# The order of the output products and the state products in the third step of a chunk of RWKV-7 time mixing

## The chip, the cores and the metric

The kernel runs on one core of a Trainium2 chip (trn2). The metric is the device time of one execution in microseconds (us). Engines are named as the profile names them: PE is TensorE's matmuls, PEld its weight loads, DVE is VectorE, ACT is ScalarE, POOL is GpSimd, SP is SyncE, which issues DMAs.

## What is computed

The reference is a trunk of two layers on 256 tokens of width 2048: a layer of RWKV-7 time mixing with a squared-ReLU MLP, then a layer of band attention with another MLP. The change lies in the time mixing alone. For each of 32 heads of 64 channels a 64 by 64 state S runs over the tokens, and each token reads it:

```python
def step(S, inp):
    r_t, w_t, k_t, v_t, kk_t, a_t = inp
    sa = jnp.einsum('bhvk,bhk->bhv', S, -kk_t)
    S = (S * w_t[:, :, None, :] + sa[..., None] * (kk_t * a_t)[:, :, None, :]
         + v_t[..., None] * k_t[:, :, None, :])
    y = jnp.einsum('bhvk,bhk->bhv', S, r_t)
    return S, y
```

`y` is then normalized per head, gated, and projected by `w_o`.

## The kernel before

**Chunks in place of tokens.** Two heads fill 128 partitions and make a pair; there are 16 pairs. The 256 tokens are cut into four chunks of 64 (`c` = 0 to 3). Within a chunk the recurrence is solved with matrices: `early` makes decays and scaled keys, `invert` builds and inverts a triangular 64 by 64 matrix per chunk (32 by 32 products at line 111, transposes on VectorE at line 239, sums at 254), and `late` (line 266) walks through the four chunks in order, since each needs the state that the chunk before left.

**The three steps of a chunk in `late`.** Each `yield` ends a step.

- First step: `g` = `mk`·`vp` (line 280) plus, from the second chunk on, the old state's part `kr`·`zs` (line 283). ScalarE copies `g` out (284).
- Second step: the inverse times `g` (287). ScalarE copies it out, negated, as `sa` (288).
- Third step: the new state and the output. The state, for chunks 0 to 2: `bk`·`vp` (293) and `bk`·`sa` (295) add up in one place, and VectorE makes `zs` from it: a plain copy in chunk 0 (298), the old state times the decay `pc` plus the products in chunks 1 and 2 (300). The output of the chunk: `vp`·`mk` (304), the old state times `kr` from chunk 1 on (307), and `sa`·`ar` (309) add up in `py`.

Every product is done for the two heads of the pair, one after the other.

**Where the results lie.** One tile `lt` (line 271, two buffers, so two pairs have one each) holds everything of a pair's `late`. It has 128 partitions and 2 × 256 float32: the first half holds `pch`, in which `g`, the second step's result and the state's products have 64 columns each, and the second half holds `py`, 64 columns for each chunk. Thus the state's products, which `zs` reads, and the output lie in the two halves of one tile.

**What sets the order on TensorE.** Slots (line 871 on). In each slot every live pair does one step: first the pairs that are in `invert`, then those in `late`, the oldest first, then those in `early`. Two pairs are in `late` at a time, 8 steps apart. Then come four blocks of the dense projections of a later pair (`proj_steps`; lines 412 and 413, 512 and 256 columns wide), or of the output projection in the last slots (401 to 403). Three slots in four end with a step of the modulation (`ada`, line 454: VectorE adds a 128 by 1024 tile that a DMA brought). A block under `tc.issue_after(x)` gets an order: its instructions on the engine of `x` stand behind `x` in that engine's queue. With it each pair's step is put behind the last TensorE instruction of the one before, and the dense blocks behind the last step. In the third step, line 302 puts the output products behind the last state product:

```python
with b.tc.issue_after(ins.ins) if c < 3 else nullcontext():
    for K in heads:
        mm(ch(py)[K, c, :], vp[K, c, :], mk[K, c, C:P], start=True, stop=False)
```

**What else VectorE does meanwhile.** Dense weights arrive as float32 and are split into two halves, the high one by ScalarE (378) and the low one by VectorE (381, 128 by 1024 elements each); three buffers of each. VectorE also does most of `early` (lines 132 to 185), the masks of `invert` (212, 227, 263) and the modulation's sums (454). It works its queue in order.

**Waits between engines** are put in by the framework where two instructions touch the same tile.

## Time and profile before

| what | value |
|---|---|
| median of three runs | 2723.46 us (2720.56 to 2725.22) |
| the profiled execution, time | 2723.2 us |
| the profiled execution, span | 2721.4 us |
| mean granted TensorE clock | 0.989 |
| PE busy | 2614.4 us |
| DVE busy | 2104.5 us |
| ACT busy | 1345.5 us |
| first to last product of line 304 | 287.3 to 764.6 us |

The span goes from the first to the last instruction of the program. The profile gives, for groups of instructions of one line, engine and shape, the count, the busy time, the mean duration, and behind a second bar the idle time of the engine just before them with what ended it. In a table of waits, "A <- B: t, n, m" reads: A's engine stood idle for t us in n places, m the longest, until B was done. `out<-in` are the names of tiles. Matmuls are pipelined, so that rows of TensorE overlap by up to some tenths of a microsecond. A float32 product of 64 by 64 shows as two instructions.

### The profile page before, as it was taken

The numbers are of one execution on the slowest core, as the hardware profiler recorded it, in microseconds if no ns is written. First come the engines' busy times: TensorE is split into PE (matmuls) and PEld (weight loads), VectorE is DVE, ScalarE is ACT, GpSimd is POOL, SyncE is SP. The second block draws the span as 40 slices with busy tenths as digits, with TensorE's granted clock in tenths as the row PEclk, the third lists the DMA queues.
The fourth block names the chain that finished last, engine by engine and source line by source line (L and its number), as shares of the span: only waits on it lengthen the run. The fifth ranks groups of instructions, "written<-read, shape, count | busy, mean of one in ns | idle before, by whom it ended". The sixth has DMA issues, their size and how long they took to land.

```text
span 2721.4 us, 58341 instructions
## 1 busy us (share of the span) xinstructions
PE 2614.4 (96%) x23690; PEld 2233.9 (82%) x23690; DVE 2104.5 (77%) x3109; ACT 1345.5 (49%) x2432; POOL 200.1 (7%) x320
## 2 busy tenths in 40 slices
PE   6999899889999999999999999999999999999997
PEld 3777677777789888888888898877898888888886
DVE  5778778777878988888888898899988555556555
ACT  3345444445456535446355554465565364453554
POOL 0002222222110000000000100000100000000002
PEclk8999999999999999999999999999999999999999
DMA  9966545554686989988899769987857555555553
GB/s 332 315 227 214 175 158 186 177 162 154 210 278 212 327 325 331 344 320 310 310 326 327 254 207 323 334 273 256 289 185 269 188 189 187 187 186 192 187 187 123
DMA packets 217390, 662.64 MB, mean 243 GB/s; under 512 B 21408, under 2 KB 68896, under 8 KB 217120
## 3 DMA queue, kind: packets, MB, share of 16 engines
q1 hardware_dynamic: 215056, 656.36, 70.0%
q8 instruction: 186, 3.05, 0.5%
q10 hardware_dynamic: 2064, 2.54, 0.3%
q14 instruction: 84, 0.69, 0.1%
HBM read 656.72 MB, written 2.10 MB: 242 GB/s over the span
## 4 chain that ended last, share of the span: by engine, by line
PE 69%; DVE 1%; DMA 1%; issue 0%; ACT 0%; DVEq 0%; ACTq 0%; SPq 0%
PE pj L412 41%; PE pj L413 21%; PE pj L402 2%; PE pj L401 2%; PE pj L403 2%; DMA rada<-w_ada 1%; PE m L476 0%; PE pT L1102 0%; DVE acc L454 0%; PE po L1109 0%; DVE wL L381 0%; PE S L1081 0%; PE o L401 0%; PE S L1080 0%; PE o L403 0%; PE o L402 0%
## 5 line engine op out<-in xcount | busy, mean ns | idle before, releaser
L381 DVE TENSOR_TENSOR wL<-raw,wH 128x1024 fp32r<-128x1024 f32 x772 | 939.7, 1218 | 355.2 <-ACT wH L378 347.5
L378 ACT CAST wH<-raw 128x1024 fp32r<-128x1024 f32 x772 | 805.9, 1045 | 825.4 <-PE pj L412 666.1
L412 PE MATMUL pj<-aHL,wH 128*128 128x512 f32 x3328 | 1205.8, 404 | 2.2 <-DVE x L927 1.4
L413 PE MATMUL pj<-aHL,wL 128*128 128x256 f32 x3328 | 938.0, 282 | 0.4 <-DVE wL L381 0.4
L412 PEld LDWEIGHTS pj<-aHL,wH 128*128 128x128 f32 x3328 | 631.1, 190 | 155.2 <-issue 9.4
L412 PE MATMUL pj<-hHL,wH 128*128 128x512 f32 x2048 | 721.4, 398 | 0.0
L413 PEld LDWEIGHTS pj<-aHL,wL 128*128 128x128 f32 x3328 | 631.5, 190 | 3.1 <-issue 0.8
L413 PE MATMUL pj<-hHL,wL 128*128 128x256 f32 x2048 | 573.5, 280 | 0.0
L412 PEld LDWEIGHTS pj<-hHL,wH 128*128 128x128 f32 x2048 | 384.5, 188 | 93.7 <-DVE hHL L973 0.2
L413 PEld LDWEIGHTS pj<-hHL,wL 128*128 128x128 f32 x2048 | 386.6, 189 | 0.1
L454 DVE SCALAR_TENSOR_TENSOR acc<-rada,ct,acc 128x1024 f32<-128x1024 f32 x256 | 327.5, 1279 | 9.4 <-DMA rada<-w_ada 8.9
L518 POOL TENSOR_TENSOR ss<-ss,sq 128x256 f32<-128x256 f32 x56 | 54.6, 975 | 1590.8 <-ACT sq L517 1590.5
L998 DVE SCALAR_TENSOR_TENSOR x<-pj,mod,x 128x256 f32<-128x256 f32 x256 | 123.3, 482 | 58.1 <-PE pj L413 54.4
L454 DVE SCALAR_TENSOR_TENSOR acc<-raw,ct,acc 128x1024 f32<-128x1024 f32 x104 | 136.7, 1315 | 27.3 <-DMA raw<-w_ada 27.0
L401 PE MATMUL pj<-aHL,wH 128*128 128x258 f32 x384 | 109.0, 284 | 0.0
L402 PE MATMUL pj<-aHL,wH 128*128 128x258 f32 x384 | 108.9, 284 | 0.0
L403 PE MATMUL pj<-aHL,wL 128*128 128x258 f32 x384 | 108.0, 281 | 0.0
L970 ACT ACTIVATE t<-t 128x256 f32<-128x256 f32 x112 | 46.8, 418 | 122.9 <-DVE t L942 122.9
L403 PEld LDWEIGHTS pj<-aHL,wL 128*128 128x128 f32 x384 | 73.2, 191 | 0.2
L402 PEld LDWEIGHTS pj<-aHL,wH 128*128 128x128 f32 x384 | 72.6, 189 | 0.1
L401 PEld LDWEIGHTS pj<-aHL,wH 128*128 128x128 f32 x384 | 72.2, 188 | 0.2
L304 PE MATMUL lt<-mk,vp 64*64 64x64 f32 x256 | 21.9, 247 | 42.8 <-DVE zs L300 30.2
(244 smaller groups left out, 2849.2 us busy)
## 6 DMA issues: line engine op xcount, KB each, us to landing
raw<-w_up SPq DMA_DIRECT2D x256, 512.0 KB, 4.0
raw<-w_down SPq DMA_DIRECT2D x256, 512.0 KB, 4.2
rada<-w_ada SPq DMA_DIRECT2D x209, 512.0 KB, 5.7
raw<-w_ada SPq DMA_DIRECT2D x111, 512.0 KB, 4.4
rawa<-w_ada SPq DMA_DIRECT2D x64, 512.0 KB, 6.6
rada<-w_ada_kv SPq DMA_DIRECT2D x64, 512.0 KB, 6.2
raw<-w_k SPq DMA_DIRECT2D x32, 512.0 KB, 4.3
raw<-w_r SPq DMA_DIRECT2D x32, 512.0 KB, 4.6
```

The costliest lines, as they stand in the source:

```text
L304: mm(ch(py)[K, c, :], vp[K, c, :], mk[K, c, C:P], start=True, stop=False)
L378: nc.scalar.copy(Hf, raw)
L381: eng.tensor_tensor(out=Lf, in0=raw, in1=Hf, op=ALU.subtract)
L401: nc.tensor.matmul(ps, H[:, i, :], a(kt)[:, 0, :], start=(first and kt == 0), stop=False)
L402: nc.tensor.matmul(ps, H[:, i, :], a(kt)[:, 1, :], start=False, stop=False)
L403: ins = nc.tensor.matmul(ps, L[:, i, :], a(kt)[:, 0, :], start=False, stop=(last and kt == KT - 1))
L412: nc.tensor.matmul(ps, H[:, i, :], a(kt), start=(kt == 0), stop=False)
L413: ins = nc.tensor.matmul(ps[:, 0, :], L[:, i, :], a(kt)[:, 0, :], start=False, stop=(kt == KT - 1))
L454: nc.vector.scalar_tensor_tensor(out=self.acc, in0=raw, scalar=ck, in1=self.acc, op0=ALU.mult, op1=ALU.add)
L518: (eng or nc.gpsimd).tensor_tensor(out=self.ss, in0=self.ss, in1=sq, op=ALU.add)
L970: nc.scalar.activation(t, t, AF.Relu)
L998: nc.vector.scalar_tensor_tensor(out=x, in0=ps[:, i, :], scalar=self.mods[(layer, 5)][:, n:n + 1], in1=x, op0=ALU.mult, op1=ALU.add)
```

## The change

In the third step of chunks 0 to 2 the output's three groups of products come first, and the state's two products second, with an `issue_after` that puts them behind the last output product. Between the two state products the order is swapped as well (`sa` first, `vp` second). `zs` is made on VectorE by the same instruction as before, after the state's products. The variable that held the old state is no longer needed, since `zs` is replaced at the end of the step. In chunk 3 the output products stand alone, as before. The number of instructions, their shapes, the tiles and their buffers are the same.

```diff
             yield
-            old = zs
+            for K in heads:
+                mm(ch(py)[K, c, :], vp[K, c, :], mk[K, c, C:P], start=True, stop=False)
+            if c:
+                for K in heads:
+                    mm(ch(py)[K, c, :], zs[K, :], kr[K, c, C:P], start=False, stop=False)
+            for K in heads:
+                ins = mm(ch(py)[K, c, :], sa[K, :], ch(ar)[K, c, :], start=False, stop=True)
             if c < 3:
-                for K in heads:
-                    mm(pch[K, 2, :], bk[K, 1, c, :], vp[K, c, :], start=True, stop=False)
-                for K in heads:
-                    ins = mm(pch[K, 2, :], bk[K, 0, c, :], sa[K, :], start=False, stop=True)
-                zs = pw.tile([P, C], F32, tag="zs", bufs=4, name="zs")
+                with b.tc.issue_after(ins.ins):
+                    for K in heads:
+                        mm(pch[K, 2, :], bk[K, 0, c, :], sa[K, :], start=True, stop=False)
+                    for K in heads:
+                        mm(pch[K, 2, :], bk[K, 1, c, :], vp[K, c, :], start=False, stop=True)
+                zn = pw.tile([P, C], F32, tag="zs", bufs=4, name="zs")
                 if c == 0:
-                    nc.vector.tensor_copy(zs, pch[:, 2, :])
+                    nc.vector.tensor_copy(zn, pch[:, 2, :])
                 else:
-                    nc.vector.scalar_tensor_tensor(out=zs, in0=old, scalar=pc[:, c, :], in1=pch[:, 2, :],
+                    nc.vector.scalar_tensor_tensor(out=zn, in0=zs, scalar=pc[:, c, :], in1=pch[:, 2, :],
                                                    op0=ALU.mult, op1=ALU.add)
-            with b.tc.issue_after(ins.ins) if c < 3 else nullcontext():
-                for K in heads:
-                    mm(ch(py)[K, c, :], vp[K, c, :], mk[K, c, C:P], start=True, stop=False)
-                if c:
-                    for K in heads:
-                        mm(ch(py)[K, c, :], old[K, :], kr[K, c, C:P], start=False, stop=False)
-                for K in heads:
-                    mm(ch(py)[K, c, :], sa[K, :], ch(ar)[K, c, :], start=False, stop=True)
+                zs = zn
             yield
```

## The prediction

> **What bounds the kernel now.** I read the page first, for the share of each engine; then the table by stages; then the waits of TensorE in the stage that the change touches; then the order of time around single waits.

> The page's head, its busy row and its row of granted clock:

> ```profile
> span 2721.4 us, 58341 instructions
> ...
> PE 2614.4 (96%) x23690; PEld 2233.9 (82%) x23690; DVE 2104.5 (77%) x3109; ACT 1345.5 (49%) x2432; POOL 200.1 (7%) x320
> ...
> PEclk8999999999999999999999999999999999999999
> ```

> TensorE (PE) is busy 96% of the span. The changed lines run from about 287 to 765 us, so I cut the span there (columns: length, then busy us and instructions of each engine, granted clock, share of the DMA engines, GB/s):

> ```profile
> 270.00:770.00 500.00, 449.18 (x8937) 368.10 (x8937) 387.03 (x712) 230.36 (x646) 106.72 (x161) 0.97 0.55 177
> 770.00:2721.40 1951.40, 1932.33 (x12557) 1687.64 (x12555) 1522.52 (x2008) 1002.58 (x1577) 67.17 (x122) 1.00 0.73 256
> ```

> In the time-mixing stage TensorE idles 500.0 − 449.2 = 50.8 us, at a clock of 0.97, while VectorE (DVE) has 113 us free and the DMAs move 177 GB/s where the later stages move 256. After it TensorE is busy 99%. So time saved in the stage should reach the end. Weight loads and modulation steps are issued by count and not by time, so none of them is skipped or added.

> Nearly all of that idle time has one cause. TensorE's waits in the stage (total, times, longest):

> ```profile
> PE lt L304 <- DVE zs L300: 30.2, 29, 3.3
> PE lt L304 <- DVE zs L298: 12.6, 15, 2.1
> PE iv L111 <- DVE tt L239: 7.0, 7, 4.5
> ```

> 44 of the 48 third steps with a state (three chunks of 16 pairs) stop at line 304, for 42.8 us in all. Line 304 multiplies `mk` by `vp` and needs no `zs`. It shares one thing with the VectorE instruction that makes `zs`: the tile `lt`, whose first half zs reads and whose second half 304 writes. The same step in the order of time, once long and once of middle length (us of start, length; the bracket is the idle time before; each x4 is two heads' products in two instructions each):

> ```profile
> 330.77 0.33 PE L293 MATMUL lt<-vp,bk 64*64 64x64 f32 x4
> 330.94 0.28 PE L295 MATMUL lt<-sa,bk 64*64 64x64 f32 x4
> 334.32 0.33 PE L304 MATMUL lt<-mk,vp 64*64 64x64 f32 x4 [3.10 <-DVE zs L300]
> ...
> 338.43 0.33 PE L280 MATMUL lt<-vp,mk 64*64 64x64 f32 x4
> ...
> 365.87 0.33 PE L304 MATMUL lt<-mk,vp 64*64 64x64 f32 x4 [1.14 <-DVE zs L300]
> ...
> 366.36 0.50 PE L412 MATMUL pj<-aHL,wH 128*128 128x512 f32 x1
> ...
> 368.61 0.33 PE L280 MATMUL lt<-vp,mk 64*64 64x64 f32 x4
> ```

> VectorE in the first of these two:

> ```profile
> 330.94 0.28 DVE L254 TENSOR_TENSOR u<-u,iv 128x128 f32<-128x128 f32 x1
> 331.33 1.17 DVE L227 TENSOR_TENSOR u<-u,csts 128x128 f32<-128x128 f32 x1
> 332.42 0.49 DVE L239 STREAM_TRANSPOSE tt<-u 128x128 f32<-128x128 f32 x2
> 332.84 1.24 DVE L454 SCALAR_TENSOR_TENSOR acc<-raw,ct,acc 128x1024 f32<-128x1024 f32 x1
> 334.00 0.27 DVE L300 SCALAR_TENSOR_TENSOR zs<-zs,pc,lt 128x64 f32<-128x64 f32 x1
> ```

> zs itself takes 0.27 us. The rest of the 3.10 is work of other pairs and of the modulation that stood ahead of it in VectorE's queue. TensorE has its next dense products ready and stands still.

> **The change, part by part.** *Moved on TensorE.* The three groups of lines 304, 307 and 309 go ahead of 293 and 295. No instruction is added or dropped, none issues a DMA, and nothing passes a queue other than TensorE's and, behind it, VectorE's. The new first product must wait for what 293 waits for today, the scalar copy `sa` out of the same tile, a step earlier. That wait is nothing (idle before it, after the last bar: 0.0; line 280 stands here for later):

> ```profile
> L280 PE MATMUL lt<-vp,mk 64*64 64x64 f32 x256 | 19.8, 230 | 0.0
> ...
> L293 PE MATMUL lt<-vp,bk 64*64 64x64 f32 x192 | 15.3, 236 | 0.0
> ```

> The swap of the two state products costs nothing: both have had their inputs for a step.

> *Removed: the wait at 304.* −42.8 us. What is late next is zs for the first product of the same pair's next chunk, line 280. From 304 to that 280 TensorE has 368.61 − 365.87 = 2.74 us of other work (the output products, the dense products, the inverse of another pair). That is the cover. Of the 44 waits only two are longer, this 3.10 and the 3.3 of the table of waits; they keep 0.36 and 0.56, so 0.9 us comes back there.

> *Removed with it: clock.* Stretches at half clock follow the long waits. Three of the seven that begin within 1.7 us of the end of such a wait (the first, the fifth and the last), the sum over all seven, and the wait ahead of the fifth:

> ```profile
> 335.02:338.43 3.41, 3.41 (x56) 2.62 (x56) 1.04 (x3) 1.62 (x3) 1.77 (x3) 0.50 0.49 154
> ...
> 546.65:550.06 3.41, 3.41 (x24) 2.64 (x19) 1.28 (x1) 0.37 (x1) 0.00 (x0) 0.50 0.60 202
> ...
> 713.90:717.31 3.41, 3.41 (x72) 3.00 (x72) 1.28 (x4) 1.31 (x3) 0.00 (x0) 0.50 0.16 60
> sum 23.89, PE 23.55 PEld 18.93 DVE 12.71 ACT 7.06 POOL 10.35; mean PE 3.36 PEld 2.70 DVE 1.82 ACT 1.01 POOL 1.48
> ```

> ```profile
> 546.17 0.33 PE L304 MATMUL lt<-mk,vp 64*64 64x64 f32 x4 [1.45 <-DVE zs L298]
> ```

> What one costs is read from the two steps above: 304 to 280 takes 338.43 − 334.32 = 4.11 us with such a stretch inside and 2.74 without, so 1.37 us; seven make 9.6 us.

> [...]

> *Added: a later zs.* The three output groups take 366.36 − 365.87 = 0.49 us, and zs can start that much later, 48 times: at most 23.5 us on VectorE, if it always stood ready for zs. Nothing on TensorE sees it inside the cover of 2.74. Below zero it cannot go, since zs never comes earlier in the step. Queued behind zs on VectorE stand the weights' low halves (line 381), the modulation sums (454) and the inverse's transposes (239); TensorE waits for the last of these, 7.0 us today.

> *Given back: VectorE is tighter.* Its work does not shrink while the stage does. Its own waits in the stage:

> ```profile
> DVE wL L381 <- ACT wH L378: 26.2, 16, 2.7
> DVE acc L454 <- DMA raw<-w_ada: 24.7, 15, 4.4
> DVE u L254 <- PE iv L111: 14.5, 10, 3.3
> ```

> Without 42.8 + 9.6 = 52.4 us the stage would be 447.6 long. Work and DMA waits alone are 387.0 + 24.7 = 411.7, 92% of that. A queue so full will be late somewhere. How much of the gain returns is the term I have to choose. It is bounded below by the 0.9 above, and above by all of it. What guides me is the shape of the 44 waits. 23 of them last 0.31 to 0.51 us, 9.8 in all; the first and the last of the 23:

> ```profile
> 287.31 0.48 PE L304 MATMUL lt<-mk,vp 64*64 64x64 f32 x4 [0.39 <-DVE zs L298]
> ...
> 747.13 0.33 PE L304 MATMUL lt<-mk,vp 64*64 64x64 f32 x4 [0.51 <-DVE zs L298]
> ```

> That is little more than zs's own 0.27 and the hand-over, so VectorE had nothing queued ahead of it, and these cannot come back under a cover of 2.74. The other 21 sum to 42.8 − 9.8 = 33.0. A single one is covered too, but the lag that TensorE's stop used to clear now stays in the queue, and two in a row can exceed the cover. I let a third return, 11.0 us, and two of the seven half-clock stretches with it, 2 × 1.37 = 2.7.

> *The sum.* 42.8 + 9.6 − 11.0 − 2.7 = 38.7 us less. The profiled execution took 2723.2 us, 1.8 more than its span; the median of the three runs is 2723.46, 0.3 above it. 2723.46 − 38.7 = 2684.8; I say 2685.

> **The rivals.** *VectorE becomes the bound.* Say that none of its waits for data and casts shrinks, that each later zs costs it in full, and that its waits for the inverse's products stay: 387.0 + 24.7 + 26.2 + 23.5 + 14.5 = 475.9 us for the stage, a gain of 24, so 2699. For it: 92% above. Against: the casts themselves wait for TensorE to free a weight buffer, 63.2 of their 78.6 us, and that should shrink as TensorE runs on:

> ```profile
> L378 ACT CAST wH<-raw 128x1024 fp32r<-128x1024 f32 (+1 forms) x63 | 64.6, 1025 | 78.6 <-PE pj L412 63.2 <-PE o L402 10.7 <-DMA raw<-w_o 3.4
> ```

> *The wait only moves.* Line 280 of the next chunk writes the same tile that zs reads, so it must wait for zs as 304 does now; if VectorE's queue is always as late, the 42.8 us appear at 280 and at 111, the stretches at half clock stay, and the time stays 2723. [...] Against the rival stands the cover, which 42 of 44 waits fit into. That the order on TensorE stays as it was would give the same time; the new program names the order of the two blocks outright, so I give that little.

> *Slower.* VectorE runs in order. If it stands at zs waiting for products that now come 0.49 us later, 381, 454 and 239 behind it come later too, and the inverse's next product (line 111) and 280 pay. With every old wait back at 280 and all 48 delays passed on: 2723.5 + 23.5 = 2747. It decides from the point at which zs lags its products by more than 2.74 us in most chunks; in this trace 2 of 48 do. VectorE stood at zs for line 295 only 8 times:

> ```profile
> DVE zs L300 <- PE lt L295: 3.1, 8, 0.8
> ```

> **How the numbers follow.** A measurement of this kernel can tell about 0.2%, 5.4 us, from no change. The forecast, a gain of 30 to 52 us: 0.62. VectorE the bound, a gain of 6 to 30: 0.24. The wait moves, within 5.4 us: 0.07. Slower: 0.07. So faster 0.86, same 0.07, slower 0.07. The low end is the whole 52.4 without any return, 2671, and 3 us below for the waits at line 111, 7.0 us today, of which some could go with the rest: 2668. The high end is past the VectorE rival's own 2699, to a gain of 15.5, which leaves out about a third of that case: 2708. About 0.8 of the chance lies inside.

> **What would show it.** On TensorE the order in a third step should read output products, `sa` product, `vp` product, and no idle time at the first of them. The row of waits at the old line 304 should be gone. Line 280's wait for zs and line 111's for `tt` should together be new by about 11 us, and hold no single wait over 2 us except a few. The clock of the stage should go from 0.97 to about 0.99. VectorE's busy time in the stage should stay at 387 us in some 461 us. The stages after it should keep their 1951 us. I am wrong if line 280 shows 44 waits of about a microsecond, if VectorE's idle time at zs for its products grows from 3.1 towards 23 us and TensorE's waits at 111 with it, or if the stage shrinks and the later stages grow by as much.

## The result, and the profile after

| | before | after |
|---|---|---|
| median, same chip | 2722.01 us (4 runs) | 2672.84 us (4 runs) |
| ratio | 1 | 0.9817, 95% interval 0.9800 to 0.9834 |
| span of the profiled execution | 2721.4 us | 2672.0 us |
| granted clock, whole span | 0.989 | 0.994 |

The change makes the kernel 49 us faster. The prediction was 2685 us with a range of 2668 to 2708.

The page of the changed kernel, its busy row and clock row:

```profile
PE 2600.1 (97%) x23690; PEld 2225.4 (83%) x23690; DVE 2101.0 (79%) x3109; ACT 1343.9 (50%) x2432; POOL 209.7 (8%) x320
...
PEclk9999999999999999999999999999999999999999
```

The instructions are the same in number, and every engine's busy time is nearly what it was. To see where the time went I cut both spans at the first and the last product into the tile `lt`; the stretch between them is called the stage from here on. The table by stages of the kernel before, then of the changed one (length, then busy us and instructions of PE, PEld, DVE, ACT and POOL, granted clock, share of the DMA engines, GB/s):

```profile
276.10:765.10 489.00, 439.00 (x8766) 359.04 (x8755) 379.61 (x697) 225.28 (x634) 102.04 (x155) 0.97 0.54 176
765.10:2721.40 1956.30, 1937.23 (x12592) 1692.38 (x12592) 1524.09 (x2011) 1004.55 (x1582) 67.17 (x122) 1.00 0.73 256
```

```profile
274.20:710.00 435.80, 421.18 (x8758) 348.25 (x8755) 374.73 (x696) 224.01 (x634) 111.60 (x155) 0.99 0.60 197
710.00:2672.00 1962.00, 1942.19 (x12593) 1695.04 (x12592) 1525.16 (x2013) 1004.51 (x1582) 67.26 (x122) 1.00 0.73 256
```

The stage is 489.0 − 435.8 = 53.2 us shorter. TensorE's idle time in it goes from 50.0 to 14.6 us, and its busy time from 439.0 to 421.2. What came before the stage is 1.9 us shorter, what comes after it 5.7 longer: 53.2 + 1.9 − 5.7 = 49.4.

TensorE's waits after, from 270 to 720 us:

```profile
PE iv L111 <- DVE tt L239: 8.7, 8, 4.2
PE ms L324 <- DVE s L154: 1.9, 5, 0.8
PE ms L324 <- issue: 1.4, 1, 1.4
PE lt L280 <- DVE zs L307: 1.2, 4, 0.3
```

The 42.8 us of the old line 304 (now 291) are gone. Its successor in the argument, line 280's wait for zs, is 1.2 us in all 48 places together. One step in the order of time, TensorE and then VectorE:

```profile
297.31 0.28 PE L291 MATMUL lt<-mk,vp 64*64 64x64 f32 x4
297.43 0.28 PE L294 MATMUL lt<-kr,zs 64*64 64x64 f32 x4
297.55 0.28 PE L296 MATMUL lt<-ar,sa 64*64 64x64 f32 x4
297.66 0.28 PE L300 MATMUL lt<-sa,bk 64*64 64x64 f32 x4
297.78 0.28 PE L302 MATMUL lt<-vp,bk 64*64 64x64 f32 x4
297.99 0.50 PE L412 MATMUL pj<-aHL,wH 128*128 128x512 f32 x1
...
300.24 0.33 PE L280 MATMUL lt<-vp,mk 64*64 64x64 f32 x4
```

```profile
297.96 0.28 DVE L254 TENSOR_TENSOR u<-u,iv 128x128 f32<-128x128 f32 x1
298.27 0.51 DVE L239 STREAM_TRANSPOSE tt<-u 128x128 f32<-128x128 f32 x2
298.70 0.77 DVE L145 TENSOR_TENSOR_SCAN s<-csts,s 128x256 f32<-128x256 f32 x1
299.39 0.25 DVE L307 SCALAR_TENSOR_TENSOR zs<-zs,pc,lt 128x64 f32<-128x64 f32 x1
```

VectorE is no quicker with zs than it was: here it starts 299.39 − 298.06 = 1.33 us after the end of the products. Over the 48 steps zs is done 0.92 us after that end on average before, and 1.34 us after. But TensorE goes from the last state product to the dense products within 0.21 us, and when it comes to line 280 at 300.24, zs has been done since 299.64.

### The profile page after: what moved, and what is told of

Same layout as the page of the kernel before. It is cut to its first block, busy times and chain, and to the rows that moved or that the text cites. A ratio compares the mean times of both kernels' runs of the same rounds, so it can differ in the third digit from the quotient of the medians.

```text
span 2672.0 us, 58365 instructions
## 1 busy us (share of the span) xinstructions
PE 2600.1 (97%) x23690; PEld 2225.4 (83%) x23690; DVE 2101.0 (79%) x3109; ACT 1343.9 (50%) x2432; POOL 209.7 (8%) x320
## 3 DMA queue, kind: packets, MB, share of 16 engines
q10 hardware_dynamic: 2064, 2.54, 0.3%
## 5 line engine op out<-in xcount | busy, mean ns | idle before, releaser
L381 DVE TENSOR_TENSOR wL<-raw,wH 128x1024 fp32r<-128x1024 f32 x772 | 940.9, 1220 | 342.6 <-ACT wH L378 337.8
L378 ACT CAST wH<-raw 128x1024 fp32r<-128x1024 f32 x772 | 805.5, 1045 | 801.2 <-PE pj L412 646.0
L412 PE MATMUL pj<-aHL,wH 128*128 128x512 f32 x3328 | 1201.9, 403 | 2.0 <-DVE x L927 1.1
L412 PEld LDWEIGHTS pj<-aHL,wH 128*128 128x128 f32 x3328 | 629.5, 189 | 154.1 <-issue 9.2
L412 PE MATMUL pj<-hHL,wH 128*128 128x512 f32 x2048 | 724.6, 399 | 0.0
L412 PEld LDWEIGHTS pj<-hHL,wH 128*128 128x128 f32 x2048 | 384.8, 188 | 95.7 <-DVE hHL L973 0.2
L413 PEld LDWEIGHTS pj<-hHL,wL 128*128 128x128 f32 x2048 | 387.0, 189 | 0.1
L454 DVE SCALAR_TENSOR_TENSOR acc<-rada,ct,acc 128x1024 f32<-128x1024 f32 x256 | 327.5, 1279 | 8.4 <-DMA rada<-w_ada 7.5
L454 DVE SCALAR_TENSOR_TENSOR acc<-raw,ct,acc 128x1024 f32<-128x1024 f32 x104 | 136.4, 1312 | 15.5 <-DMA raw<-w_ada 15.4
L402 PE MATMUL pj<-aHL,wH 128*128 128x258 f32 x384 | 109.0, 284 | 0.0
L970 ACT ACTIVATE t<-t 128x256 f32<-128x256 f32 x112 | 46.8, 418 | 122.6 <-DVE t L942 122.6
L402 PEld LDWEIGHTS pj<-aHL,wH 128*128 128x128 f32 x384 | 72.6, 189 | 0.1
L972 ACT ACTIVATE t<-t 128x256 f32<-128x256 f32 x128 | 53.4, 417 | 3.4
```

What stands on the lines that cost most here:

```text
L378: nc.scalar.copy(Hf, raw)
L381: eng.tensor_tensor(out=Lf, in0=raw, in1=Hf, op=ALU.subtract)
L402: nc.tensor.matmul(ps, H[:, i, :], a(kt)[:, 1, :], start=False, stop=False)
L412: nc.tensor.matmul(ps, H[:, i, :], a(kt), start=(kt == 0), stop=False)
L413: ins = nc.tensor.matmul(ps[:, 0, :], L[:, i, :], a(kt)[:, 0, :], start=False, stop=(kt == KT - 1))
L454: nc.vector.scalar_tensor_tensor(out=self.acc, in0=raw, scalar=ck, in1=self.acc, op0=ALU.mult, op1=ALU.add)
```

## The experiments

Theory: the old stop is made by the shared tile, TensorE stands at the head of its queue while VectorE is late, and any order that puts 2.7 us of other TensorE work between the state products and the next product into that tile takes the stop away, with its loss of clock. Rivals: the order itself matters (what is early or late in the step), the stop is one for data, or the gain is limited by VectorE's total work.

No run leaves out any of the computation. The times are medians in us. The stage's figures are cut as above; half clock is the time in the stage at which the clock stood at half. They are of one execution of each kernel, and the half-clock time differs between executions: the granted clock over the whole span is 0.987 to 0.993 in those of the kernel before, 0.992 to 0.995 in those of the changed one.

| run | time | ratio to before, 95% interval | stage | TensorE idle in it | half clock |
|---|---|---|---|---|---|
| before | 2721 to 2724 | 1 | 489.0 | 50.0 | 30.7 |
| after | 2672.8 | 0.9817 (0.9800 to 0.9834) | 435.8 | 14.6 | 6.8 |
| c0_only | 2718.8 | 0.9982 (0.9972 to 0.9992) | 479.4 | 42.8 | 34.1 |
| c12_only | 2692.8 | 0.9890 (0.9870 to 0.9910) | 454.1 | 26.6 | 17.1 |
| no_swap | 2674.0 | 0.9817 (0.9801 to 0.9833) | 436.6 | 15.8 | 6.8 |
| next_first | 2738.3 | 1.0052 (1.0034 to 1.0071) | 500.2 | 60.4 | 30.7 |
| half_cover | 2699.5 | 0.9924 (0.9909 to 0.9939) | 461.1 | 23.1 | 13.7 |
| cross | 2682.5 | 0.9859 (0.9838 to 0.9881) | 448.1 | 22.3 | 13.7 |
| defer | 2674.5 | 0.9823 (0.9807 to 0.9839) | 439.7 | 18.9 | 3.4 |
| before_zs4 | 2867.0 | 1.0525 (1.0504 to 1.0546) | 630.8 | 135.6 | 184.3 |
| after_zs4 | 2714.3 | 0.9966 (0.9952 to 0.9980) | 475.6 | 41.3 | 34.1 |
| after_dup | 2684.8 | 0.9867 (0.9850 to 0.9883) | 444.2 | 22.2 | 10.2 |
| after_again | 2676.6 | 0.9833 (0.9819 to 0.9847) | 436.5 | 15.6 | 6.8 |
| act_copies | 2668.2 | 0.9799 (0.9784 to 0.9813) | 427.2 | 9.0 | 0 |

### Is it the tile or the order? cross

```diff
-        bank = pp.tile([P, 2, T], F32, tag="lt", bufs=2, name="lt")
-        pch, py = bank[:, 0, 0:3 * C].rearrange("p (a t) -> p a t", a=3), bank[:, 1, :]
+        banks = [b.lts[j % 2], b.lts[1 - j % 2]]
+        pch, py = banks[0][:, 0, 0:3 * C].rearrange("p (a t) -> p a t", a=3), banks[1][:, 1, :]
...
+            self.lts = [pp.tile([P, 2, T], F32, tag=f"lt{i}", bufs=1, name="lt") for i in range(2)]
```

> The old order on TensorE, but a pair's state products and its output lie in two different tiles (of two tiles, each holds one pair's first half and the other pair's second half). If the shared tile made the wait, the waits at line 304 for zs go without any change of order, 42.8 us to under 5, and the half-clock stretches with them; new waits between the two pairs that now share a tile may cost up to about 1 us for each pair's last steps, 16 us: 2672 to 2692 us. If the old order itself is the cause, the waits at 304 stay and the time is 2722 us.

The order in the third step is that of the kernel before. TensorE's waits:

```profile
PE iv L111 <- DVE tt L239: 8.7, 7, 4.5
PE lt L280 <- DVE sl L320: 8.3, 6, 3.7
PE lt L304 <- ACT sa L288: 4.3, 10, 0.4
```

No wait for zs is left at line 304, and the time falls to 2682.5 without any product being moved. So the shared tile makes the stop. The two other rows are the price expected: two pairs now share a tile, and one pair waits for ScalarE or VectorE to read the other's half.

### Is it the work between? next_first and half_cover

Both take the changed kernel and issue line 280 of the next chunk earlier; from the second chunk on it no longer stands in its old place.

```diff
...
+                with b.tc.issue_after(ins.ins):
+                    for K in heads:
+                        mm(pch[K, 0, :], mk[K, c + 1, 0:C], vp[K, c + 1, :], start=True, stop=False)
             yield
...
```

> The changed kernel, with the next chunk's product of mk and vp (line 280) issued right behind the state's products, in the same step, ahead of the dense products. It doesn't need zs as data; it writes the half of lt that zs reads, in other columns. If a product into the tile that zs reads has to wait for zs, and the gain comes from the 2.74 us of dense work between, the stops return at this product: about 40 us of waits, half-clock stretches again, 2712 to 2728 us. If the gain came from the output products being early, or the old wait was one for data, it stays near 2673 us.

The moved product is line 313 there. The waits for it:

```profile
PE lt L313 <- DVE zs L308: 34.4, 27, 3.5
PE lt L313 <- DVE zs L306: 16.5, 15, 2.2
```

The stop is back in full, at a product that has no use for zs: 50.9 us in 42 places. It is 8.1 us more than the 42.8 of the kernel before, and the time is 2738, 10 us above the range I gave. The output products now stand ahead of the state products and delay zs without hiding it. Without a cover the new order is slower than the old one.

In half_cover the same product stands behind the first half of the slot's dense products:

```diff
-                with tc.issue_after(last):
-                    for _ in range(todo):
-                        next(dense, None)
+                for i in range(max(todo, 1)):
+                    with tc.issue_after(last):
+                        if i < todo:
+                            next(dense, None)
+                    last = self.last_pe()
+                    if i == 0:
+                        for first in self.between:
...
```

> As next_first, but the next chunk's product of mk and vp stands in the middle of the slot's dense products, behind the first two of four blocks (about 0.7 us of them) in place of none. In the changed kernel zs is done 0.55 to 2.76 us after the start of the last state products; with a cover of about 0.95 us the parts of these times above it sum to about 33 us, less where another pair's step adds cover. So the waits at this product should fall from 51 us to 20 to 35, and the time lie between the changed kernel and next_first, 2698 to 2720 us. If the wait depended on the order alone and not on the cover, it would be that of next_first, 2738, or of the changed kernel, 2673.

```profile
PE lt L313 <- DVE zs L308: 10.6, 12, 1.4
PE lt L313 <- DVE zs L306: 1.8, 4, 0.5
```

12.4 us, less than the 20 to 35 expected: from the start of the last state product to the moved product TensorE has 1.31 us of work on average (1.05 to 2.67) and not the 0.95 I took. With the cover going from none over half to whole, the wait goes 50.9, 12.4, 1.2. The time of 2699.5 is higher than that wait explains: TensorE's busy time in the stage is 438.0 against 421.2. One part is two more stretches at half clock. The rest lies where the dense run is cut in two. From the start of the instruction before the moved product to the start of the one behind it takes 0.49 us on average, idle time taken out; around line 280 in the changed kernel it is 0.25. Over the 48 that makes 12 us.

### Is it that zs is later, or the swap? defer and no_swap

In defer the state products stay first, and the output products of chunks 0 to 2 go into the next step, behind line 283:

```diff
+                with b.tc.issue_after(ins.ins):
+                    outputs()
             nc.scalar.copy(g, pch[:, 0, :])
...
```

> State products first as in the old order, and the output products of chunks 0 to 2 a whole slot later, behind the first products of the next chunk. It takes the stop away as the change does, by the dense work between, but zs isn't made later. If the later zs costs nothing, the time is that of the changed kernel, 2673 us within 5; if the 0.49 us of later zs is felt (up to 23.5 us in 48 steps), it is faster than the changed kernel by several us.

In no_swap the changed kernel adds `vp`'s product first and `sa`'s second:

```diff
-                        mm(pch[K, 2, :], bk[K, 0, c, :], sa[K, :], start=True, stop=False)
+                        mm(pch[K, 2, :], bk[K, 1, c, :], vp[K, c, :], start=True, stop=False)
...
-                        mm(pch[K, 2, :], bk[K, 1, c, :], vp[K, c, :], start=False, stop=True)
+                        mm(pch[K, 2, :], bk[K, 0, c, :], sa[K, :], start=False, stop=True)
```

> The changed kernel, but with the state's two products in their old order (vp first, sa second). Both have their inputs a step earlier, so my theory expects no difference from the changed kernel: 2673 us within 3. If the swap were part of the gain (sa's product standing first so that something is freed earlier), it would be some us slower.

2674.5 and 2674.0 against 2672.8: both are the changed kernel's time. Where the cover holds, zs half a microsecond later costs nothing, and a wholly different way to the same cover gives the same gain.

### Do the parts add? c0_only and c12_only

The new order stands under `if c == 0:` in one kernel and `if c in (1, 2):` in the other; the old order stands in the `else`.

> The new order in chunk 0 alone; chunks 1 and 2 keep the old one. If each wait is a stop of TensorE for its own zs, and half-clock stretches belong to the waits ahead of them, the parts add up: the 15 waits for line 298 go (12.6 us) and two of the seven stretches (2 x 1.37 us), a gain of about 15 us, near 2707 us, with the waits of chunks 1 and 2 unchanged at about 30 us. The rival, that VectorE's lag only goes on to the next stop, expects the waits of chunks 1 and 2 to grow by most of the 12.6 and a gain under 6 us.

> The new order in chunks 1 and 2 alone. By the sum of parts the 29 waits for line 300 go (30.2 us) and five half-clock stretches (5 x 1.37 us): a gain of about 37 us, near 2685 us; together with the chunk-0 run it should give the 49 us of the whole change within 5 us. By the rival that the lag goes on to the next stop the 15 waits of chunk 0 grow well above 12.6 us and the gain is under 25.

The waits for zs that are left, of c0_only and then of c12_only:

```profile
PE lt L326 <- DVE zs L322: 31.9, 29, 2.8
```

```profile
PE lt L326 <- DVE zs L320: 14.8, 15, 2.2
```

The parts do not add. The gains against before are 5 us (2723.9 − 2718.8) and 31, in sum 36, where I expected 15 and 37 and the whole gives 49. In the traces the two stages are 9.6 and 34.9 us shorter, where the whole gives 53.2, so 8.7 us are missing. Of these 4.8 are idle time of TensorE (7.2 + 23.4 against 35.4), most of it the waits for zs that stay and grow by 1.7 and 2.2 us: the lag does go on to the next stop, though by far less than the rival has it. The other 3.9 are busy time (2.4 + 11.5 against 17.8), and there the clock tells. c0_only has taken 12.6 us of waits away and has no fewer half-clock stretches than before (34.1 us against 30.7); c12_only has still three that are not in the changed kernel. The stretches do not belong to certain waits, as I had assumed in counting seven of them. The rest of the 13 us between 36 and 49 lies between executions and is not placed; the ten executions of c0_only have granted clocks from 0.985 to 0.992.

### How much more could VectorE be late? before_zs4, after_zs4 and after_dup

In the first two, the instruction that makes zs is done four times over:

```diff
+                for _ in range(4):
+                    if c == 0:
...
```

> The kernel before with the same instruction done four times over. Here TensorE stands still until zs is done, so each of the 48 stops grows by the three added instructions, about 0.6 us: 29 us more at line 304, and more half-clock stretches at 1.37 us each: 2750 to 2765 us. If the stops were not on the path that sets the end, it stays at 2722 us.

> The changed kernel with the VectorE instruction that makes zs done four times over in place of once (same result): about 3 x 0.2 us more on VectorE and zs later by as much, 48 times, near 30 us of VectorE's time in the stage (382.8 us busy becomes about 412). With a cover of 2.74 us and slack on VectorE, TensorE sees little: up to 8 us more than the changed kernel, near 2677 us. If VectorE were nearly the bound at 92% of the stage, as my prediction feared, most of the 30 us shows: 2690 to 2705 us.

Both are far above what I expected, and a reading of the trace says why. VectorE in after_zs4, around one zs:

```profile
495.40 0.22 DVE L306 COPY zs<-lt 128x64 f32<-128x64 f32 x1
495.54 1.27 DVE L455 SCALAR_TENSOR_TENSOR acc<-raw,ct,acc 128x1024 f32<-128x1024 f32 x1
496.73 0.22 DVE L306 COPY zs<-lt 128x64 f32<-128x64 f32 x1
496.86 0.28 DVE L254 TENSOR_TENSOR u<-u,iv 128x128 f32<-128x128 f32 x1
497.06 0.22 DVE L306 COPY zs<-lt 128x64 f32<-128x64 f32 x1
497.19 0.30 DVE L239 STREAM_TRANSPOSE tt<-u 128x128 f32<-128x128 f32 x1
497.42 0.18 DVE L306 COPY zs<-lt 128x64 f32<-128x64 f32 x1
```

The framework put other work between the four. From the start of the first to the end of the last it takes 2.06 us on average over the 48 (2.32 in before_zs4) where one zs takes 0.25. So these runs make zs 1.8 and 2.1 us later, not 0.6. Read that way they say more. In the old order most of it is stop: of 48 × 2.1, about 100 us, TensorE's idle time shows 135.6 − 50.0 = 85.6, and 45 more stretches at half clock come with it. In the new order TensorE reaches line 283 on average 1.37 us after zs is done (from the 48 pairs of times in the changed kernel's trace). With zs 1.8 us later, the parts by which the 48 fall short sum to 28 us; the wait at line 280 became 33.8:

```profile
PE lt L280 <- DVE zs L308: 25.7, 16, 3.1
PE lt L280 <- DVE zs L306: 8.1, 9, 2.2
```

So the changed kernel's cover is about half used, and another 1.8 us of lag uses it up in 25 of the 48 places.

In after_dup the load is put elsewhere: lines 170, 172, 174 and 175 of `early` stand twice.

```diff
...
         nc.vector.tensor_tensor(out=self.kh, in0=km, in1=e2, op=ALU.mult)
+        nc.vector.tensor_tensor(out=self.kh, in0=km, in1=e2, op=ALU.mult)
```

> The changed kernel with four VectorE instructions of each pair's first steps (lines 170, 172, 174 and 175, about 0.42 us each) done twice, same result: 64 x 0.42 = 27 us more on VectorE, about as much as the run that made zs four times over added (28.8 us busy), but none of it between a chunk's state products and its zs. If what counts is how late zs is after its products, TensorE sees little: under 10 us more than the changed kernel, 2674 to 2683 us. If VectorE's total work is the bound, the 27 us show, near 2700 us or above, as they did there (2714).

TensorE's waits for VectorE in it:

```profile
PE iv L111 <- DVE tt L243: 14.8, 11, 5.5
...
PE lt L284 <- DVE zs L311: 1.7, 4, 0.7
```

At 2684.8 it is 12 and 8 us slower than the changed kernel's two medians (2672.8 and 2676.6), between the two expectations. VectorE's busy time in the stage rises by 19 us (374.7 to 394.0; the rest of the added work lies ahead of the stage or overlaps), the stage by 8.4, and the stage begins 6 us later, I take it because the first pairs' steps follow one from the other. The wait for zs hardly moves; the inverse's transposes take the delay. VectorE's total is thus not free, but it is not the bound either.

### A version that is faster than both: act_copies

```diff
-                    nc.vector.tensor_copy(zn, pch[:, 2, :])
+                    nc.scalar.copy(zn, pch[:, 2, :])
...
-                    nc.vector.tensor_copy(uf[K, :, H:C], pi[K])
+                    nc.scalar.copy(uf[K, :, H:C], pi[K])
```

> The changed kernel with two small copies out of PSUM moved from VectorE to ScalarE: chunk 0's zs (3.5 us in all) and the inverse's last corner (line 258, 9.1 us). VectorE loses 12.6 us of 375, ScalarE gains about as much of 231. The run with 19 us more on VectorE in the stage made the stage 8.4 us longer, 0.44 us for each; by that this one should be about 5 us faster than the changed kernel, near 2668. If the cost of that run was its place, the first steps of a pair, and not VectorE's total, no difference: 2673 within 3. If ScalarE's queue (casts of 1.05 us) makes the copies later, slower by some us.

> The changed kernel itself once more, beside the run above on the same chip and in more rounds: 2673 us within 3, and the waits at line 280 for zs again near 1 us in all.

2668.2 against 2676.6 for the changed kernel beside it, 8 us faster; the two intervals do not overlap. The changed kernel itself came out just above the range given for it, and its waits at line 280 for zs are 2.1 us and not 1. The waits of act_copies from 262 to 720 us:

```profile
PE iv L111 <- DVE tt L239: 5.9, 13, 1.2
...
PE lt L280 <- DVE zs L307: 1.8, 4, 0.8
```

The reason I gave, 0.44 us for each microsecond taken off VectorE, is not shown by it. The longest wait at line 111, near 280 us and 3.9 to 5.5 us long in every other kernel here (4.3 in after_again), is gone, and so are the two stretches at half clock behind it: 4.3 − 1.2 + 2 × 1.37 = 5.8 of the 8 us. In the changed kernel's trace six VectorE instructions stand between the sum of line 254 and that transpose, one of them the 1.22 us of a line 381; here four do, and line 381 comes behind it. Whether it is the smaller load or this one place in the order was not separated.

## Why the prediction was right, and where its terms were off

**The cause of the stop: right, and shown.** cross takes the sharing away and the stop of 42.8 us at line 304 goes; next_first brings back a product that shares the tile and the stop returns, 50.9 us at line 313.

**The cover: right in kind, read 0.49 us too long.** It is what the gain depends on: 50.9, 12.4 and 1.2 us of waits with none, half and all of it. But the 2.74 us, read from line 304 on, hold the 0.49 of the output products, which the change puts ahead of the state products; by the same lines 2.25 was left. In the changed kernel it is 2.57 us on average from the end of the last state product to line 280 (0.84 to 4.22), and zs is done 1.34 us after that end, 2.54 at the latest.

**The wait removed, 42.8 us: right.** Nothing of it is left at its place.

**Clock, 9.6 us: right in size, wrong in its book-keeping.** All seven stretches went; the two that are left in the stage follow the long wait at line 111, as two did before. But they are not owned by single waits, as c0_only showed.

**A term that I left out.** The stops cost more than their idle time. From the start of the last state product to the start of whatever TensorE does next, the 48 steps take 53.4 us before and 4.4 after. Of these 49.0 us 43.1 are idle time; the other 5.9 are the end of the last product. In the changed kernel's step above (297.31 to 297.78 us) one group of small products follows the other after 0.11 to 0.12 us, though each takes 0.28 to finish; at a stop the rest stands bare, and the profile counts it as busy. TensorE's busy time in the stage fell by 17.8 = 9.6 + 5.9 + 2.3; the 2.3 are not placed.

**The part given back: mis-sized.** This was the term that I said I chose, 11.0 us of waits and 2.7 of clock. In the stage 14.6 − (50.0 − 42.8) = 7.4 us of idle time came back and no half-clock stretch. Line 280's wait for zs is 1.2 of it, and line 111's for `tt` goes from 6.2 to 8.2, where I had looked for about 11 in the two. So the stage's sum is 42.8 + 9.6 + 5.9 + 2.3 − 7.4 = 53.2. The forecast gain of 38.7 and the 49.4 of the two profiled spans differ by 6.3 (13.7 of return that became 7.4), the 8.2 left out, 1.9 ahead of the stage and −5.7 behind it. Both misses of the sum are towards more gain; that the later stages took some of it back was not forecast, and it brought the time nearer to the one I gave.

I had feared VectorE's queue at 92%; but VectorE's own waits made room, as one sentence against that rival had it. VectorE's waits in the stage after:

```profile
DVE wL L381 <- ACT wH L378: 14.6, 19, 2.0
DVE acc L454 <- DMA raw<-w_ada: 14.5, 13, 2.0
DVE u L254 <- PE iv L111: 7.2, 5, 2.9
```

These three were 63.4 us in the stage before and are 36.3. The sign given for the slower case did not come either: VectorE's idle time at zs for its products is 2.8 us after, 3.1 before.

**That the later stages keep their time: not quite.** They took 5.7 us more. 1.1 of it is a longer wait for a weight's low half at the start of the output projection (1.9 before, 3.0 after) and about 1.4 a half-clock stretch right behind it. The other 3.2 are not placed. From kernel to kernel this part takes 1955.9 to 1963.0 us here, and the six with the shortest stages all lie above 1961, so it need not be chance.

**The rivals.** That the wait only moves holds without cover alone. Slower is what next_first is, where zs is late and the stop is there too. VectorE as the bound was not reached by the change; after_dup, 19 us busier on VectorE and 8.4 us longer in the stage, shows that it is not far.

## What to carry to other kernels

When an engine waits for something that it does not need, look for the tile that both touch, and put the products that must wait for the reader as far behind it as there is other work: first what nobody reads soon, then what the slow engine reads, then the dense work. Measure the cover in the trace (from the last product to the next one into the same tile) and the lag of the reader, and compare the two place by place and not by their means. The stops of TensorE cost here 42.8 us of idle time, 5.9 us of the ends of the last products and an estimated 9.6 us of clock, and the gain came only over the whole and not part by part: 5 and 31 us for its two parts, 49 for both together.

## What the runs showed of the hardware

What such a stretch costs was 1.37 us in the prediction's one pair of steps. before_zs4 gives an estimate over many: the stage is 141.8 us longer than before, 85.6 of them idle, and the other 56.2 with 45 more stretches make 1.25 us each. At that price the seven would have been 8.8 us in place of 9.6.
